# Matrix sums of a fast product moved to GpSimd, and six more chunks done as seven products

## The chip, the cores and the metric

One core of one Trainium2 chip runs the whole program. The metric is the device time of one execution in microseconds. The kernel before was timed in three runs.

## What is computed

A float32 network of three layers on 256 tokens of width 1024. The first block is feed-forward, hybrid mixer (neighbourhood attention and pooling, gated), feed-forward and a gated per-layer embedding; the second block has two layers, each with feed-forward, a mixer and feed-forward again. The first mixer of the second block is gated linear attention, the second is retention. Six feed-forward layers in all (f1, f2, s0 to s3), with hidden width 2816:

```
def swiglu(x, w_gate, w_up, w_down):
    return (jax.nn.silu(x @ w_gate) * (x @ w_up)) @ w_down

def gla_mixer(x, w_in, w_gate, b_gate, norm_g, w_out):
    q, k, v, r, g_low = split_cols(x @ w_in, GLA_SPLITS)
    log_a = log_sigmoid(g_low @ w_gate + b_gate) / GLA_TAU
    o = rms_norm_2(gla_chunked(q, k, v, log_a), norm_g)
    return (o.reshape(bsz, l, GLA_VAL) * silu(r)) @ w_out
```

Every layer ends in a residual with a normalisation, so it has to be complete before the next one begins.

## The kernel before

The 256 tokens are two tiles of 128. Activations are kept transposed (128x512 is four blocks of 128 input features for one tile) and are the stationary operand; weights stream. To get float32 accuracy, each operand is split into a high half in the fast float32 format and the rest: for weights, ScalarE casts `whi` from `raw` (L174, L196) and VectorE subtracts `wlo = raw - whi` (L177, L197). Each product is three matmuls (hi hi, hi lo, lo hi; L217 to L219), all 128x128 by 128x512.

The weights come in **units** of 128x2048 (1 MB), loaded on SP's queue, in the order of a plan that is written down once (`all_units`). A unit of a projection has four blocks of 128 rows and 512 columns. `fetch` loads and splits one; `unit` hands it to the code that uses it, and sees that the units behind it are fetched ahead (four ahead near a group of seven products). There are five buffers each for `raw`, `whi` and `wlo`, used in turn. A unit used plainly costs TensorE 2 tiles x 4 blocks x 3 = 24 matmuls.

The feed-forward layer (`ffn`) goes through its hidden columns in chunks of 512: chunks 0 to 4 with two gate units and two up units each, a chunk 5 of 256 columns, and then the down projection of 11 units (`lagged`). Some chunks are done as **seven products** (`seven`, Winograd's form of Strassen's scheme): the four weight units of a chunk are a 2x2 matrix of blocks a, b, c, d, the two tiles and the two halves of the input features the other, and seven products of 12 matmuls stand in for eight. Before, these are chunks 2 and 4 of layers f2 and s0 to s3 (`SEVEN`), the mixer's gate columns (two groups) and two pairs of retention's columns. Each product needs its own matrix: some are units, some sums of units. `fetch_sum` makes the sums in place in the `raw` buffers, one VectorE operation at L194 each, and splits the result. The seven results are added up on VectorE (L392 to L402); in the feed-forward layer the sums then give the gate, through ScalarE's Silu, and the hidden product `pr` (L476). `sums_in` makes the four differences of the inputs (`xr`, L307) and their splits.

The seven products and the plain ones are made in the same five PSUM buffers (`mm`), in turn: a product starts when the fifth product before it has been read. Work that comes later (transposes of the hidden product, for one) is put off by a count of matmul steps (`defer`, `tick`). The order on each engine is set when the program is built, and each engine then goes through its own list.

GpSimd does small things: the normalisations' powers (L247, L262, L341), the scaling of the residual (L354), the gate product of the linear attention (L799) and retention's rotation (L944, L945).

Of the kernel before, what the change touches and what calls it, by code (L numbers as in the profile page):

```python
# [35 lines left out]
SUMS = (("a", None), ("a", "b"), ("b", "c"), ("a", "c"), ("c", None), ("d", None), ("a", "d"))  # L36
# [36 lines left out]
SEVEN = (2, 4)  # L73
MIX_ORDER = [1, 0, 2, 3, (4, 5), (6, 7)]
GLA_ORDER = [1, 0, 2, 4, 3, 5]
# [16 lines left out]
class Build:  # L92
# [89 lines left out]
    def fetch_sum(self, four, j):  # L182


        nc = self.nc
        if j == 0:
            self.sums = {}
        r = self.sums
        for key, at in {0: (("a", 0), ("b", 2)), 2: (("c", 3),), 5: (("d", 1),)}.get(j, ()):
            r[key] = self.T("raw", [P, UNIT], F32)  # L190
            nc.sync.dma_start(out=r[key], in_=self.ins[four[at][0]][four[at][1]])
        key, other = SUMS[j]
        if other:
            nc.vector.tensor_tensor(out=r[key], in0=r[key], in1=r[other], op=ALU.add)  # L194
        hi, lo = self.T("whi", [P, UNIT], F32R), self.T("wlo", [P, UNIT], F32R)
        nc.scalar.copy(hi, r[key])  # L196
        nc.vector.tensor_tensor(out=lo, in0=r[key], in1=hi.bitcast(F32), op=ALU.subtract)  # L197
        return Split(hi, lo)
# [103 lines left out]
    def sums_in(self, raws, tag):  # L302

        a11, a12, a21, a22 = (raws.pop((t, n)) for t in range(NT) for n in range(2))
        y = {}
        for i, o, a, b in ((1, a22, a21, a22), (3, a21, a11, a21), (2, a11, a11, a22), (4, a12, a12, a11)):
            self.nc.vector.tensor_tensor(out=o, in0=a, in1=b, op=ALU.subtract)  # L307
# [8 lines left out]
        return y  # L316
# [52 lines left out]
    def seven(self, x, y, four, done):  # L369
# [15 lines left out]
        p1, u2, u4, c22 = t("u", "p1"), t("u", "u2"), t("y", "u4"), t("y", "c22")  # L385
        nc.scalar.copy(p1, times("P1", x[0][0], 0))
# [62 lines left out]
    def ffn(self, xT, r, wg, wu, wd, after, first=False, raws=None):  # L449
# [19 lines left out]
        def finish7(c):  # L469
            prs = []  # L470

            def done(t, a, b):
                sg = self.T("sg", [P, CW], F32)
                pr = self.T("sg", [P, CW], F32, name="pr")
                nc.scalar.activation(sg, a, AF.Silu)
                nc.vector.tensor_tensor(out=pr, in0=b, in1=sg, op=ALU.mult)  # L476
                prs.append(pr)
                if t:
                    self.defer(4, lambda: turn(c, CW, *prs))

            return done
# [35 lines left out]
        for c in range(1, 6):  # L517
            if raws is not None and c == 1:
                self.defer(4, lambda: y.update(self.sums_in(raws, "ld")))
            if raws is not None and c in SEVEN:  # L520
                self.settle(lambda: y)
# [17 lines left out]
    class Chunks:  # L539
# [10 lines left out]
        def sums(self):  # L550
            self.y.update(self.b.sums_in(self.raws, "S"))

        def pair(self, c):

            if c not in self.groups:
                self.b.settle(lambda: self.y)

                def done(t, *outs):
                    for i in range(2):
                        self.done(c[i], t, outs[i])  # L560
                        self.over.add((c[i], t))
# [210 lines left out]
    def gla(self, xT, raws, after):  # L772
# [140 lines left out]
        whole(1), ch.go(2), glow(1), ch.go(2), logits(1)  # L913
        for work in ((decay1,), (decay2,), (decay3, 0), (decay3, 1), (k_decay, 0), (k_decay, 1), (q_decay, 0), (q_decay, 1),
                     (inner, 0), (inner, 1), (far,), (read, 0, 0), (carry, 0), (read, 0, 1, read, 1, 0, carry, 1), (), (read, 1, 1)):
# [305 lines left out]
```

## Time and profile before

| | us |
|---|---|
| median of 3 runs | 1611.38 (1611.19 to 1611.48) |
| profiled execution, its own time | 1611.8 |
| its span, first to last instruction | 1610.0 |
| TensorE busy | 1589.4 |
| VectorE busy | 1233.6 |
| ScalarE busy | 836.7 |
| GpSimd busy | 107.3 |

The span is the profiled execution without what lies around it. Busy times are sums over the instructions of an engine; matmuls overlap, and so do operations that follow one another on VectorE by a little, so that a row's duration is not always the distance to the next start. In the rows below, a line is `start, duration, engine, source line, operation, output<-inputs, shapes`; a bracket at the end gives the idle time before it and what ended that.

### The profile page before, as it was taken

The numbers are of one execution on the slowest core, as the hardware profiler recorded it, in microseconds if no ns is written. First come the engines' busy times: TensorE is split into PE (matmuls) and PEld (weight loads), VectorE is DVE, ScalarE is ACT, GpSimd is POOL, SyncE is SP. The second block draws the span as 40 slices with busy tenths as digits, with TensorE's granted clock in tenths as the row PEclk, the third lists the DMA queues.
The fourth block names the chain that finished last, engine by engine and source line by source line (L and its number), as shares of the span: only waits on it lengthen the run. The fifth ranks groups of instructions, "written<-read, shape, count | busy, mean of one in ns | idle before, by whom it ended". The sixth has DMA issues, their size and how long they took to land. (4 is left out here: it accounts for less than half of the span.)

```text
span 1610.0 us, 18253 instructions
## 1 busy us (share of the span) xinstructions
PE 1589.4 (99%) x7353; PEld 1307.2 (81%) x7353; DVE 1233.6 (77%) x1086; ACT 836.7 (52%) x831; POOL 107.3 (7%) x102
## 2 busy tenths in 40 slices
PE   9999999999999999999999999999999999999997
PEld 6888877788888888888888888888887888788886
DVE  6654688978993789947648996699938899799954
ACT  7443555755663665634645563456634464456531
POOL 0000000000000100001022000100003401010000
PEclk9999999999999999999999999999999999999999
DMA  9764533654574455556534556544754543655550
GB/s 346 289 212 155 209 121 128 235 184 155 191 273 166 175 211 209 208 205 221 181 123 155 185 182 233 193 176 183 279 185 160 190 183 115 246 200 189 184 191 27
DMA packets 49797, 308.11 MB, mean 191 GB/s; under 512 B 6048, under 2 KB 7328, under 8 KB 15024
## 3 DMA queue, kind: packets, MB, share of 16 engines
q1 hardware_dynamic: 49568, 306.93, 52.6%
q8 instruction: 58, 0.95, 0.2%
q14 instruction: 27, 0.22, 0.0%
q10 hardware_dynamic: 144, 0.00, 0.0%
HBM read 305.86 MB, written 1.05 MB: 191 GB/s over the span
## 5 line engine op out<-in xcount | busy, mean ns | idle before, releaser
L177 DVE TENSOR_TENSOR wlo<-raw,whi 128x2048 fp32r<-128x2048 f32 (+1 forms) x231 | 503.1, 2185 | 247.1 <-ACT whi L174 247.0
L174 ACT CAST whi<-raw 128x2048 fp32r<-128x2048 f32 (+1 forms) x230 | 417.5, 1824 | 332.0 <-PE acc L219 190.5
L217 PE MATMUL mm<-whi,xTh 128*128 128x512 f32 x848 | 337.5, 398 | 0.2 <-ACT xTh L234 0.2
L219 PE MATMUL mm<-whi,xTl 128*128 128x512 f32 x848 | 331.4, 391 | 0.4 <-DVE xTl L235 0.4
L218 PE MATMUL mm<-wlo,xTh 128*128 128x512 f32 x848 | 331.3, 391 | 0.0
L196 ACT CAST whi<-raw 128x2048 fp32r<-128x2048 f32 x98 | 186.9, 1910 | 119.1 <-DVE raw L194 78.0
L197 DVE TENSOR_TENSOR wlo<-raw,whi 128x2048 fp32r<-128x2048 f32 x98 | 222.6, 2286 | 8.6 <-ACT whi L196 8.6
L217 PE MATMUL acc<-whi,hTh 128*128 128x512 f32 x528 | 207.0, 392 | 0.0
L219 PE MATMUL acc<-whi,hTl 128*128 128x512 f32 x528 | 205.6, 389 | 0.0
L218 PE MATMUL acc<-wlo,hTh 128*128 128x512 f32 x528 | 205.5, 389 | 0.0
L219 PEld LDWEIGHTS mm<-whi,xTl 128*128 128x128 f32 x848 | 159.2, 188 | 35.8 <-DVE xTl L235 1.8
L217 PEld LDWEIGHTS mm<-whi,xTh 128*128 128x128 f32 x848 | 159.3, 188 | 32.6 <-issue 0.8
L218 PEld LDWEIGHTS mm<-wlo,xTh 128*128 128x128 f32 x848 | 159.5, 188 | 31.1
L194 DVE TENSOR_TENSOR raw<-raw 128x2048 f32<-128x2048 f32 x56 | 128.3, 2291 | 0.1
L219 PEld LDWEIGHTS acc<-whi,hTl 128*128 128x128 f32 x528 | 99.1, 188 | 20.9
L218 PEld LDWEIGHTS acc<-wlo,hTh 128*128 128x128 f32 x528 | 99.2, 188 | 20.1
L217 PEld LDWEIGHTS acc<-whi,hTh 128*128 128x128 f32 x528 | 99.1, 188 | 20.1
L217 PE MATMUL mm<-whi,xh 128*128 128x512 f32 x176 | 69.0, 394 | 2.2 <-ACT whi L174 1.7
L218 PE MATMUL mm<-wlo,xh 128*128 128x512 f32 x176 | 68.8, 391 | 0.0
L219 PE MATMUL mm<-whi,xl 128*128 128x512 f32 x176 | 68.6, 390 | 0.0
L234 ACT CAST hTh<-hT 128x512 fp32r<-128x512 f32 (+1 forms) x72 | 38.6, 546 | 56.0 <-PE hT L226 55.8
L217 PE MATMUL P<-whi,xTh 128*128 128x512 f32 x168 | 66.3, 395 | 0.0
(261 smaller groups left out, 2105.5 us busy)
## 6 DMA issues: line engine op xcount, KB each, us to landing
raw<-in_rin SPq DMA_DIRECT2D x24, 1024.0 KB, 4.8
raw<-in_bin SPq DMA_DIRECT2D x16, 1024.0 KB, 4.8
raw<-in_f2g SPq DMA_DIRECT2D x12, 1024.0 KB, 4.8
raw<-in_s0g SPq DMA_DIRECT2D x12, 1024.0 KB, 4.8
raw<-in_gin SPq DMA_DIRECT2D x12, 1024.0 KB, 4.8
raw<-in_s1g SPq DMA_DIRECT2D x12, 1024.0 KB, 4.8
raw<-in_s2g SPq DMA_DIRECT2D x12, 1024.0 KB, 4.8
raw<-in_s3g SPq DMA_DIRECT2D x12, 1024.0 KB, 5.1
```

The source lines that it names most:

```text
L174: nc.scalar.copy(hi[:, s], raw[:, s])
L177: nc.vector.tensor_tensor(out=lo[:, s], in0=raw[:, s], in1=hi[:, s].bitcast(F32), op=ALU.subtract)
L194: nc.vector.tensor_tensor(out=r[key], in0=r[key], in1=r[other], op=ALU.add)
L196: nc.scalar.copy(hi, r[key])
L197: nc.vector.tensor_tensor(out=lo, in0=r[key], in1=hi.bitcast(F32), op=ALU.subtract)
L217: mm(ps, x.hi, w.hi, start=start, stop=False)
L218: mm(ps, x.hi, w.lo, start=False, stop=False)
L219: mm(ps, x.lo, w.hi, start=False, stop=stop)
L234: self.nc.scalar.copy(hi, v)
```

## The change

1. **Sums on GpSimd.** `fetch_sum` splits first and then adds on GpSimd (`nc.gpsimd.tensor_tensor`, new line L196), in place in the `raw` buffers. The products change their order: P1, P2, P5, P3, P7, P6, P4 with the matrices a, d, a+b, c, b+c, a+b+c, a+b+c+d. All four units of a group are now loaded with its first two products.
2. **Order of the results.** `seven` adds up in the new order (L389 to L407) and hands over each of the four results as it is complete.
3. **Input differences on GpSimd** (L316), with their splits put off by two to five steps.
4. **A third chunk:** `SEVEN` is now (2, 3, 4), so chunks 2, 3 and 4 of five feed-forward layers follow one another as groups.
5. **Linear attention:** the gate columns 4 and 5 become one group, ahead of the second half of the values (3), and the last work items are spread over the products differently.

```
-SUMS = (("a", None), ("a", "b"), ("b", "c"), ("a", "c"), ("c", None), ("d", None), ("a", "d"))
-SEVEN = (2, 4)
+SEVEN = (2, 3, 4)
-GLA_ORDER = [1, 0, 2, 4, 3, 5]
+GLA_ORDER = [1, 0, 2, (4, 5), 3]
...
-        for key, at in {0: (("a", 0), ("b", 2)), 2: (("c", 3),), 5: (("d", 1),)}.get(j, ()):
+        for key, at in {0: (("a", 0), ("b", 2)), 1: (("d", 1), ("c", 3))}.get(j, ()):
             r[key] = self.T("raw", [P, UNIT], F32)
             nc.sync.dma_start(out=r[key], in_=self.ins[four[at][0]][four[at][1]])
-        key, other = SUMS[j]
-        if other:
-            nc.vector.tensor_tensor(out=r[key], in0=r[key], in1=r[other], op=ALU.add)
+        src = r["adacbad"[j]]
         hi, lo = self.T("whi", [P, UNIT], F32R), self.T("wlo", [P, UNIT], F32R)
-        nc.scalar.copy(hi, r[key])
-        nc.vector.tensor_tensor(out=lo, in0=r[key], in1=hi.bitcast(F32), op=ALU.subtract)
+        nc.scalar.copy(hi, src)
+        nc.vector.tensor_tensor(out=lo, in0=src, in1=hi.bitcast(F32), op=ALU.subtract)
+        for o, i in {0: ("ab",), 1: ("bc",), 2: ("ac", "da")}.get(j, ()):
+            nc.gpsimd.tensor_tensor(out=r[o], in0=r[o], in1=r[i], op=ALU.add)
...
-        for i, o, a, b in ((1, a22, a21, a22), (3, a21, a11, a21), (2, a11, a11, a22), (4, a12, a12, a11)):
-            self.nc.vector.tensor_tensor(out=o, in0=a, in1=b, op=ALU.subtract)
...
+        for n, (i, o, a, b) in enumerate(((1, a22, a21, a22), (3, a21, a11, a21), (2, a11, a11, a22), (4, a12, a12, a11))):
+            self.nc.gpsimd.tensor_tensor(out=o, in0=a, in1=b, op=ALU.subtract)
+            self.defer(2 + n, lambda i=i, o=o: split(i, o))
...
+        u2, c11, c12, c22 = t("u", "u2"), t("u", "c11"), t("y", "c12"), t("y", "c22")
+        nc.scalar.copy(u2, times("P1", x[0][0], 0))
         yield
-        p5 = times("P5", y[1], 1)
+        TT(out=c11, in0=times("P2", x[0][1], 1), in1=u2, op=ALU.add)
+        done(0, 0, c11)
         yield
-        p7 = times("P7", y[3], 2)
+        self.settle(lambda: len(y) == 4)
+        p5 = times("P5", y[1], 2)
         yield
-        TT(out=u2, in0=times("P6", y[2], 3), in1=p1, op=ALU.subtract)
-        TT(out=u4, in0=p5, in1=u2, op=ALU.add)
-        TT(out=c22, in0=u4, in1=p7, op=ALU.subtract)
+        p3 = times("P3", y[4], 3)
+        yield
+        p7 = times("P7", y[3], 4)
+        yield
+        TT(out=u2, in0=times("P6", y[2], 5), in1=u2, op=ALU.subtract)
+        TT(out=c12, in0=p5, in1=u2, op=ALU.add)
+        TT(out=c22, in0=c12, in1=p7, op=ALU.subtract)
         TT(out=u2, in0=u2, in1=p7, op=ALU.subtract)
-        yield
-        TT(out=u4, in0=times("P3", y[4], 4), in1=u4, op=ALU.add)
-        yield
-        TT(out=p1, in0=times("P2", x[0][1], 5), in1=p1, op=ALU.add)
-        done(0, p1, u4)
+        TT(out=c12, in0=p3, in1=c12, op=ALU.add)
+        done(0, 1, c12)
+        done(1, 1, c22)
         yield
         TT(out=u2, in0=times("P4", x[1][1], 6), in1=u2, op=ALU.subtract)
-        done(1, u2, c22)
+        done(1, 0, u2)
...
-        whole(1), ch.go(2), glow(1), ch.go(2), logits(1)
+        whole(1), ch.go(2), glow(1), ch.go(1), self.defer(4, ch.sums), ch.go(1), logits(1)
```

**VectorE, between two groups of layer s1.** Before, from the last splits of chunk 2's group into plain chunk 3 (`L197` splits a matrix of a group, `L177` a plain unit; P_6900 is P6, P_6845 P5, P_6882 P7, P_6923 P3, P_6943 P2):

```order
L197 TENSOR_TENSOR wlo<-raw,whi 128x2048 x3
L235 TENSOR_TENSOR hTl<-hT,hTh 128x512
L177 TENSOR_TENSOR wlo<-raw,whi 128x2048
L235 TENSOR_TENSOR hTl<-hT,hTh 128x512
L392 TENSOR_TENSOR u_6824<-P_6900,p_6823 128x512
L177 TENSOR_TENSOR wlo<-raw,whi 128x2048
L393 TENSOR_TENSOR u_6825<-P_6845,u_6824 128x512
L177 TENSOR_TENSOR wlo<-raw,whi 128x2048
L394 TENSOR_TENSOR c_6826<-u_6825,P_6882 128x512
L395 TENSOR_TENSOR u_6824<-u_6824,P_6882 128x512
L397 TENSOR_TENSOR u_6825<-P_6923,u_6825 128x512
```

And now, from chunk 2's group into chunk 3's (`L194` is now the split of a group's matrix; P_7022 is P6, P_6961 P5, P_7000 P7, P_6978 P3, P_7048 P4; the row of three is the last split of chunk 2 and the first two of chunk 3):

```order
L194 TENSOR_TENSOR wlo<-raw,whi 128x2048 x3
L399 TENSOR_TENSOR u_6901<-P_7022,u_6901 128x512
L194 TENSOR_TENSOR wlo<-raw,whi 128x2048
L400 TENSOR_TENSOR c_6903<-P_6961,u_6901 128x512
L194 TENSOR_TENSOR wlo<-raw,whi 128x2048
L401 TENSOR_TENSOR c_6904<-c_6903,P_7000 128x512
L402 TENSOR_TENSOR u_6901<-u_6901,P_7000 128x512
L403 TENSOR_TENSOR c_6903<-P_6978,c_6903 128x512
L407 TENSOR_TENSOR u_6901<-P_7048,u_6901 128x512
L484 TENSOR_TENSOR pr<-c_6903,sg 128x512
```

The operations that read P5 (L400) and P3 (L403) stand behind the splits of the third and the fourth matrix of the next group, which before were splits of plain units. The third matrix is a sum.

**GpSimd, around one feed-forward layer of the second block (s1 and s2 look alike).** Before, GpSimd had only the normalisations there (two `rl` and four scalings for each layer's end):

```order
L341 TENSOR_TENSOR rl<-mv,mhalf 128x1
L354 TENSOR_SCALAR h_86<-y 128x512 x2
L341 TENSOR_TENSOR rl<-mv,mhalf 128x1
L354 TENSOR_SCALAR h_87<-y 128x512 x2
L341 TENSOR_TENSOR rl<-mv,mhalf 128x1
```

And now, behind the same operations of one layer's end and ahead of those of the next:

```order
L355 TENSOR_SCALAR h_87<-y 128x512 x2
L316 TENSOR_TENSOR xr<-xr 128x512 x4
L196 TENSOR_TENSOR raw<-raw 128x2048 x12
L342 TENSOR_TENSOR rl<-mv,mhalf 128x1
L355 TENSOR_SCALAR h_86<-y 128x512 x2
```

Each feed-forward layer has four input differences and then twelve sums there, four for each group, each waiting for the split that reads the buffer before it is overwritten. Over the program there are 80 sums at L196 where there were 56 at L194, 331 splits of 128x2048 where there were 313, and 6396 matmuls of split operands where there were 6468.

## Rows read from the trace of the kernel before

**Rows 1.** The page, busy us, share of the span and instructions of three engines.
```profile
PE 1589.4 (99%) x7353; PEld 1307.2 (81%) x7353; DVE 1233.6 (77%) x1086; ACT 836.7 (52%) x831; POOL 107.3 (7%) x102
```

**Rows 2.** Busy time by engine in stretches: mixer, linear attention, third feed-forward layer, parts, retention.
```profile
core 0: us, PE busy (x) PEld busy (x) DVE busy (x) ACT busy (x) POOL busy (x), PEclk, DMA share, GB/s
205.00:350.00 145.00, 140.90 (x690) 113.97 (x690) 124.30 (x123) 81.80 (x106) 0.55 (x1) 0.99 0.46 170
765.00:855.00 90.00, 90.00 (x446) 74.19 (x445) 52.12 (x54) 49.48 (x67) 11.89 (x16) 1.00 0.42 146
872.00:1036.00 164.00, 164.00 (x748) 135.83 (x748) 127.32 (x98) 85.19 (x69) 0.27 (x2) 1.00 0.53 192
885.00:965.00 80.00, 80.00 (x369) 66.36 (x368) 75.46 (x51) 46.50 (x37) 0.00 (x0) 1.00 0.50 183
965.00:1036.00 71.00, 71.00 (x321) 58.74 (x320) 40.69 (x36) 28.00 (x21) 0.15 (x1) 1.00 0.61 220
1310.00:1413.00 103.00, 101.86 (x459) 82.98 (x458) 89.95 (x83) 51.44 (x44) 9.82 (x12) 1.00 0.57 208
```

**Rows 3.** Timeline of TensorE in a plain chunk: start us, duration us.
```profile
899.82 0.39 PE L217 MATMUL mm<-whi,xTh 128*128 128x512 f32 x1
900.05 0.39 PE L218 MATMUL mm<-wlo,xTh 128*128 128x512 f32 x1
...
901.64 0.39 PE L219 MATMUL mm<-whi,xTl 128*128 128x512 f32 x1
```

**Rows 4.** Groups of instructions by shape: busy us, mean ns | idle before, releasers.
```profile
L177 DVE TENSOR_TENSOR wlo<-raw,whi 128x2048 fp32r<-128x2048 f32 x215 | 493.0, 2297 | 245.5 <-ACT whi L174 245.5
L174 ACT CAST whi<-raw 128x2048 fp32r<-128x2048 f32 x215 | 408.7, 1908 | 330.5 <-PE acc L219 190.5 <-PE mm L219 62.2 <-issue 33.2
L194 DVE TENSOR_TENSOR raw<-raw 128x2048 f32<-128x2048 f32 x56 | 128.3, 2291 | 0.1
L458 DVE TENSOR_TENSOR pr<-mm,sg 128x512 f32<-128x512 f32 x30 | 20.6, 687 | 13.6 <-PE mm L219 13.4
```

**Rows 5.** Timeline of GpSimd: undisturbed two-input operations of three sizes.
```profile
805.37 1.29 POOL L799 TENSOR_TENSOR gate<-gate,gnorm 128x512 f32<-128x512 f32 x1 [0.77 <-ACT gate L798]
...
1233.53 0.72 POOL L945 TENSOR_TENSOR rot<-rb,ra 128x256 f32<-128x256 f32 x1
...
1294.28 0.56 POOL L247 TENSOR_TENSOR rr<-err,mhalf 128x1 f32<-128x1 f32 x1
```

**Rows 6.** Groups of GpSimd: all four gate products together.
```profile
L799 POOL TENSOR_TENSOR gate<-gate,gnorm 128x512 f32<-128x512 f32 x4 | 6.1, 1516 | 47.1 <-ACT gate L798 47.1
```

**Rows 7.** Timeline of VectorE and GpSimd side by side, at two places.
```profile
1037.84 3.84 POOL L354 TENSOR_SCALAR h<-y 128x512 f32<-128x512 f32 x2 [1.01 <-DVE y L349]
1038.33 2.29 DVE L177 TENSOR_TENSOR wlo<-raw,whi 128x2048 fp32r<-128x2048 f32 x1
1040.53 0.69 DVE L235 TENSOR_TENSOR xTl<-xT,xTh 128x512 fp32r<-128x512 f32 x1
...
1243.39 2.83 DVE L177 TENSOR_TENSOR wlo<-raw,whi 128x2048 fp32r<-128x2048 f32 x1
...
1247.34 5.02 DVE L177 TENSOR_TENSOR wlo<-raw,whi 128x2048 fp32r<-128x2048 f32 x2
1247.56 2.65 POOL L944 TENSOR_TENSOR rot<-ra,rb 128x256 f32<-128x256 f32 x1 [3.49 <-DVE rb L941]
1250.17 2.78 POOL L945 TENSOR_TENSOR rot<-rb,ra 128x256 f32<-128x256 f32 x1
```

**Rows 8.** Timeline of TensorE behind its longest wait.
```profile
283.94 1.98 PE L696 MATMUL py<-pl,pool_w 128*128 128x256 f32 x4 [3.54 <-ACT pl L592]
...
286.14 0.63 PE L218 MATMUL P<-wlo,xTh 128*128 128x512 f32 x1
286.56 0.63 PE L219 MATMUL P<-whi,xTl 128*128 128x512 f32 x1
```

**Rows 9.** Busy time in the 2 us behind that wait, columns as in rows 2.
```profile
284.00:286.00 2.00, 2.00 (x5) 1.64 (x6) 2.00 (x5) 0.41 (x2) 0.00 (x0) 0.52 0.00 0
```

**Rows 10.** DMA issues of the page: KB each, median us to landing.
```profile
raw<-in_s1g SPq DMA_DIRECT2D x12, 1024.0 KB, 4.8
```

More of the change, by code (lines that the diff above doesn't have):

```diff
@@ L300, in turn_in, with sums_in, split @@
         self.defer(TURN[t] + n + (more if raws is not None else 0), turn)
-    def sums_in(self, raws, tag):
+    def sums_in(self, raws, tag, y):
         a11, a12, a21, a22 = (raws.pop((t, n)) for t in range(NT) for n in range(2))
-        y = {}
-        for i, o, a, b in ((1, a22, a21, a22), (3, a21, a11, a21), (2, a11, a11, a22), (4, a12, a12, a11)):
-            self.nc.vector.tensor_tensor(out=o, in0=a, in1=b, op=ALU.subtract)
+        def split(i, o):
             if i < 3:
@@ L315, in sums_in @@
             y[i] = Split(hi, lo)
-        return y
+        for n, (i, o, a, b) in enumerate(((1, a22, a21, a22), (3, a21, a11, a21), (2, a11, a11, a22), (4, a12, a12, a11))):
+            self.nc.gpsimd.tensor_tensor(out=o, in0=a, in1=b, op=ALU.subtract)
+            self.defer(2 + n, lambda i=i, o=o: split(i, o))
     def rms_post(self, t, acc, gpost, half):
@@ L469, in finish7, with done @@
         def finish7(c):
[L470 to L479, printed above, removed]
+            got, prs = {}, {}
+            def done(t, i, ps):
+                got[t, i] = ps
+                if i == 0:
+                    sg = got[t, 0] = self.T("sg", [P, CW], F32)
+                    nc.scalar.activation(sg, ps, AF.Silu)
+                if (t, 1 - i) in got:
+                    prs[t] = pr = self.T("sg", [P, CW], F32, name="pr")
+                    nc.vector.tensor_tensor(out=pr, in0=got[t, 1], in1=got[t, 0], op=ALU.mult)
+                if t and i == 0:
+                    self.defer(4, lambda: turn(c, CW, prs[0], prs[1]))
             return done
@@ L518, in ffn @@
             if raws is not None and c == 1:
-                self.defer(4, lambda: y.update(self.sums_in(raws, "ld")))
+                self.defer(4, lambda: self.sums_in(raws, "ld", y))
             if raws is not None and c in SEVEN:
-                self.settle(lambda: y)
                 for _ in self.seven(xT, y, [(wg, 2 * c), (wg, 2 * c + 1), (wu, 2 * c), (wu, 2 * c + 1)], finish7(c)):
@@ L550, in sums, with done @@
         def sums(self):
-            self.y.update(self.b.sums_in(self.raws, "S"))
+            self.b.sums_in(self.raws, "S", self.y)
         def pair(self, c):
             if c not in self.groups:
[L556 to L561, printed above, removed]
+                def done(t, i, ps):
+                    self.done(c[i], t, ps)
+                    self.over.add((c[i], t))
                 self.groups[c] = self.b.seven(self.xT, self.y, [(self.name, 2 * i + j) for i in c for j in range(2)], done)
@@ L912, in gla @@
         whole(0), ch.go(3), glow(0), ch.go(1), logits(0)
-        whole(1), ch.go(2), glow(1), ch.go(2), logits(1)
+        whole(1), ch.go(2), glow(1), ch.go(1), self.defer(4, ch.sums), ch.go(1), logits(1)
         for work in ((decay1,), (decay2,), (decay3, 0), (decay3, 1), (k_decay, 0), (k_decay, 1), (q_decay, 0), (q_decay, 1),
-                     (inner, 0), (inner, 1), (far,), (read, 0, 0), (carry, 0), (read, 0, 1, read, 1, 0, carry, 1), (), (read, 1, 1)):
+                     (inner, 0), (inner, 1), (far,), (read, 0, 0), (carry, 0), (read, 0, 1), (read, 1, 0, carry, 1), (read, 1, 1)):
             i = 0
```

2 lines of the change are left out of this document (removed).

## Prediction

> **What bounds the kernel now.** I read the page's busy times first. TensorE is busy 1589.4 of 1610.0 us, VectorE 1233.6, GpSimd 107.3 [rows 1]. Next come the stages. In the third feed-forward layer, 872 to 1036 us, TensorE has no gap at all; but in its chunks 1 to 4, 885 to 965 us, VectorE is busy 75.46 of 80.00 us, in the 71 us of down projection behind them 40.69 [rows 2]. So TensorE sets the time, and VectorE follows so closely in just the stretch that the change rewrites. Last, a matmul's listed duration is no price: matmuls overlap, and the starts of neighbours lie 0.228 us apart (899.82 to 901.64, eight matmuls later) [rows 3]. I count that for each.
>
> **Products.** A plain chunk of four weight units costs 4 x 24 = 96 matmuls; as seven products it costs 7 x 12 = 84. Six chunks more are done so (chunk 3 in five layers, the gates once): 72 matmuls x 0.228 = **16.4 us off TensorE**, all on the path.
>
> **Splits.** Each new group splits seven matrices where four were split: 18 casts x 1.91 us on ScalarE and 18 subtractions on VectorE [rows 4]. ScalarE is busy 46.50 of 80.00 us in the stretch [rows 2], which hides its share: nothing. If that cover were gone it would be 34 us. The subtractions are in the account below.
>
> **Sums.** The 56 in-place sums at L194, 2.29 us each [rows 4], leave VectorE, and 80 appear on GpSimd (20 groups x 4). The trace has no GpSimd operation of 128x2048. An undisturbed two-input one takes 0.72 us at 128x256 and 1.29 at 128x512 [rows 5], 0.57 more for 256 columns; six more such lots give **4.7**, which I take as the nearest. Bounds: counting from the 128x1 operation at 0.56 [rows 5], 1.29 + 3 x 0.73 = 3.5; four times the mean of all four gate products (1.52) [rows 6], some of which were disturbed, 6.1. Taken alone, 4 x 4.7 = 18.8 us in a group of seven products (7 x 12 x 0.228 = 19.2 us) would just fit.
>
> **They don't run alone.** At 1247.34 two subtractions (whi from raw, both inputs in SBUF) stand on VectorE, and two rotation products on GpSimd arrive among them. The first needs 2.65 us instead of about 0.72: it waits for the running subtraction. It then runs, and the pair of subtractions takes 5.02 instead of 2 x 2.29, 0.45 more: the second one stood still until GpSimd was through; the second rotation again takes 2.78 [rows 7]. At 1037.84 a GpSimd scaling sits out the whole subtraction behind it, 3.84 us for two of them, while the subtraction takes its plain 2.29 and the xTl operation behind it, which has an input in PSUM, its plain 0.69 [rows 7]. So GpSimd and VectorE exclude each other wherever VectorE reads two operands from SBUF; with one in PSUM it doesn't. What the rows don't show is a long GpSimd operation with a subtraction arriving early in it. The longest such wait is 0.54 us (2.83 against 2.29 at 1243.39) [rows 7]. Bounds for what a sum of 4.7 us does to a waiting subtraction: 0.54 us, or all 4.7. I take all of it, because in each row VectorE stood until the GpSimd operation ended.
> The Trainium skill, page SBUF — State Buffer, section Who interferes with whom, speaks against the change in the same way: a VectorE instruction with two SBUF inputs and a GpSimd one that reads SBUF take a shared port pair in turn, and the later one blocks for the whole instruction. By that rule the sum is the one below; by waits of 0.54 us it would be that of the first rival.
>
> **Feed-forward layers.** Sums and subtractions then use one resource in turn. Per group: 7 subtractions x 2.2 (their starts back to back, 1038.33 to 1040.53 [rows 7]) + 4 sums x 4.7 + 2 operations on the hidden product, both inputs in SBUF, x 0.69 [rows 4] = 15.4 + 18.8 + 1.4 = **35.6 us, against 19.2 us of TensorE**. Before, a plain chunk (4 x 24 x 0.228 = 21.9 us of TensorE) stood between two groups and let VectorE catch up; now chunks 2, 3 and 4 follow each other. The first group can be prepared during chunk 1: five buffers of each split half allow splitting from 21.9 us before its first product, and its four sums and seven subtractions (34.2 us) end about when they are needed. The second and third can't: 2 x (35.6 - 19.2) = **33 us** of waiting.
> Walking the new order of the queues through adds to it. On VectorE the subtraction of the second group's third matrix stands ahead of the operation that frees P5's PSUM buffer, in which the next group's P1 is to be made, and one more ahead of that which frees P3's, for P2. Both subtractions wait for a sum, so TensorE first waits some 12 us at the second group's P1 and 5 at its P2, later 4 to 5 us at each of P1, P2 and the transposes of the third. Behind the third group, the raw buffer of its first matrix is held until the sixth split, so the next unit's load (4.8 us to land [rows 10]) starts late, and VectorE's queue puts three subtractions ahead of the freeing operation: up to 9 more, 42 in all. I take **36 us per layer, 180 for five**. With 3.5 us per sum the rate gives 23 (115); with 6.1, 44 (220).
>
> **Mixer and retention.** Their four groups exist already; 16 sums go from 2.29 to 4.7 us of the shared resource, 39 us. VectorE's idle time there is 145.00 - 124.30 = 20.7 us and 103.00 - 89.95 = 13.1 us [rows 2]. I take 12, bounds 0 and 39. The linear attention has room (52.12 of 90.00 us busy [rows 2]) for 3 subtractions and 4 sums, 25 us; its decay chain may wait behind a sum, and the last values are read right after they are made: 3, bounds 0 and 10.
>
> **At nothing:** the operand differences (28 of L307 on VectorE, now 32 on GpSimd at 1.29 us): they run during chunk 1, ahead of the group's sums; without that cover, 4 x 1.29 = 5.2 us a call. Also the clock: after TensorE waited 3.54 us at 283.94, the grant was 0.52 of full speed in the 2 us behind, and starts lay 0.42 apart instead of 0.228 [rows 8, 9]: 1.2 GHz for about 2 us, some 1 us lost. Where TensorE waits for sums anyway that loss is hidden; uncovered, some four such waits in five layers are 20.
>
> **Sum.** Against the profiled execution's 1611.8: - 16.4 + 180 + 12 + 3 = 1790.4; the median of the runs is 0.4 lower, so I say **1790 us**. Low ends: 1611.4 - 16.4 + 115 = 1710. High ends: 1611.4 - 16.4 + 220 + 39 + 10 + 20 = 1884.
>
> **Rivals.**
> *Faster: the exclusion costs little.* If a waiting subtraction gets in between parts of a long GpSimd operation, a sum costs VectorE at most 0.54 us. Then three groups need 21 x 2.2 of subtractions, 21 operations on products and 12 others at 0.69 (hidden products and their splits) and 12 x 0.54: 46.2 + 22.8 + 6.5 = 75.5 us, against 57.5 us of products plus some 14 us in stock (five units x 2.7): 4 us late per layer at worst, most likely 1. 1611.4 - 16.4 + 3 = **1598**. For it: four sums fit in 19.2 us; VectorE loses 56 x 2.29 = 128 us. Against: no row shows VectorE getting in. It decides between waits of under about 1 us and the whole operation. Chance 0.16. With 4 us late in each layer and little else it ends at 1611 to 1615, no change: 0.03.
> *Half.* The exclusion holds but more is prepared ahead than I count, or a sum is nearer 3 us: 10 to 20 us a layer, 1611.4 - 16.4 + 75 = **1670**. Against: buffers for five units only. Chance 0.07.
> *Worse.* The waits feed each other also in the mixers, each late PSUM buffer delaying splits by their buffers: 44 a layer and the high ends of the others, **1884** and more. Against: in the mixers, attention work on TensorE lies between. Chance 0.04.
> *The change doesn't do what it says:* the order shows 80 sums on GpSimd, none on VectorE, 72 matmuls fewer; no chance left.
>
> **How the numbers follow.** The forecast has 0.70. Over 0.2% (3.2 us, about what a measurement can tell) slower: 0.70 + 0.07 + 0.04 = 0.81; within: 0.03; faster: 0.16. The range leaves out the faster and unchanged cases (0.19) and reaches over the others: from 1640, the foot of the half case, to the high ends, 1880. The forecast's own range is 1710 to 1880.
>
> **What would show it.** In the changed profile: sums on GpSimd near 4.7 us undisturbed and near 6.9 with a subtraction ahead; subtractions up to 4.7 us longer than 2.29, alternating with sums; TensorE gaps of several us, at the second and third group of every feed-forward layer, put down to VectorE's product operations or subtractions; the layer's stretch 30 us longer, the down projection unchanged; matmuls 72 fewer at the same pitch. Wrong, if subtractions beside sums keep 2.29 to 2.9 us: then the first rival. If the sums take 4.7 but TensorE's gaps lie elsewhere, the walk is wrong and the rate right.

## The result and the profile after

The changed kernel takes **1864.43 us** (median of 4 runs, 1863.01 to 1864.99), the one before 1611.29 (1611.17 to 1611.48) beside it: a ratio of **1.157 [1.155, 1.159]**, 253 us more. The forecast was 1790, its range 1640 to 1880. Of the spans of the two profiled executions the difference is 251.2.

The page of the profile after, busy us by engine (before: [rows 1]):

```profile
PE 1650.0 (89%) x7281; PEld 1337.7 (72%) x7281; DVE 1391.0 (75%) x1066; ACT 870.7 (47%) x859; POOL 604.2 (32%) x214
```

The 72 matmuls are gone, and TensorE is still busy 61 us longer; the other 190 us of the longer span are gaps. Where the time went is read by stage, from the second layer norm's small GpSimd operation at the end of one layer to the first at the end of the next (in the first block, between the like operations of its own normalisation). Layer s1 is the third of the five feed-forward layers that the change touches (f2, s0 to s3), and is called the third one here. These two rows of GpSimd's timeline bound it, 208.53 us apart; before they stood 167.35 apart.

```profile
975.08 0.99 POOL L342 TENSOR_TENSOR rl<-mv,mhalf 128x1 f32<-128x1 f32 x1 [7.97 <-DVE mv L341]
...
1183.61 0.99 POOL L342 TENSOR_TENSOR rl<-mv,mhalf 128x1 f32<-128x1 f32 x1 [87.79 <-DVE mv L341]
```

All stages so: the five feed-forward layers are 42.3, 39.9, 41.2, 42.0 and 42.2 us longer, together **207.6**; the mixer 7.4, the linear attention 17.2, the retention 20.4, together **45.0**. The rest didn't move.

Within that layer, the whole, the stretch with the three groups and the down projection (columns as in [rows 2]):

```profile
979.00:1184.00 205.00, 173.16 (x736) 140.32 (x735) 153.99 (x96) 90.14 (x73) 76.64 (x17) 0.92 0.42 153
1006.00:1125.00 119.00, 87.19 (x348) 69.44 (x347) 103.80 (x59) 52.75 (x40) 61.49 (x11) 0.86 0.42 157
1125.00:1184.00 59.00, 58.97 (x265) 48.55 (x264) 27.26 (x23) 20.11 (x17) 0.39 (x1) 1.00 0.46 159
```

The down projection has no gap. In the 119 us ahead of it TensorE stands still for 31.8, and its granted clock has a mean of 0.86 where it was 1.00: 348 matmuls take 87.19 us, 0.251 each, against 80.00 / 369 = 0.217 in [rows 2], both stretches with 28 short transposes among them. (1.00 is 2.4 GHz; the mean lies between that and the lower level, 1.2.) The clock isn't low throughout. These two pieces, columns as above, lie behind a gap of 2.29 us and behind one of 8.22:

```profile
1036.00:1040.00 4.00, 2.97 (x12) 2.18 (x12) 0.80 (x2) 0.00 (x0) 4.00 (x1) 1.00 0.00 0
1048.00:1053.00 5.00, 4.86 (x13) 3.89 (x14) 5.00 (x1) 0.95 (x1) 4.92 (x2) 0.57 0.00 0
```

TensorE's longest groups of waits (us in total, times, longest):

```profile
PE hT L225 <- DVE pr L484: 54.3, 10, 6.4
PE P L216 <- DVE c L400: 36.2, 5, 8.2
PE P L216 <- DVE u L402: 26.7, 5, 5.6
PE mm L216 <- DVE u L399: 20.6, 5, 4.1
PE tp L225 <- DVE kend L855: 14.7, 1, 14.7
```

The first four occur once or twice in each of the five layers and all wait for VectorE. Now the two groups of instructions that share the resource (busy us, mean ns):

```profile
L196 POOL TENSOR_TENSOR raw<-raw 128x2048 f32<-128x2048 f32 x80 | 440.8, 5509 | 275.3 <-DVE wlo L194 272.2
L194 DVE TENSOR_TENSOR wlo<-raw,whi 128x2048 fp32r<-128x2048 f32 x140 | 466.9, 3352 | 67.3 <-ACT whi L193 66.9
```

A subtraction took 2.297 us before [rows 4]; these 140 take 3.35. And the passage from the first of the three groups into the second, in the timeline (start, duration; VectorE, GpSimd, ScalarE, and TensorE's waits; a row with x2 is two operations on end):

```profile
1034.08 11.15 POOL L196 TENSOR_TENSOR raw<-raw 128x2048 f32<-128x2048 f32 x2 [8.43 <-DVE wlo L194]
1036.12 0.68 DVE L399 TENSOR_TENSOR u<-P,u 128x512 f32<-128x512 f32 x1
1036.95 0.47 PE L216 MATMUL P<-whi,xTh 128*128 128x512 f32 x1 [2.29 <-DVE u L399]
...
1040.67 3.70 ACT L193 CAST whi<-raw 128x2048 fp32r<-128x2048 f32 x2 [7.94 <-POOL raw L196]
1042.60 4.79 DVE L194 TENSOR_TENSOR wlo<-raw,whi 128x2048 fp32r<-128x2048 f32 x1 [5.80 <-ACT whi L193]
...
1047.31 0.68 DVE L400 TENSOR_TENSOR c<-P,u 128x512 f32<-128x512 f32 x1
1047.47 4.54 POOL L196 TENSOR_TENSOR raw<-raw 128x2048 f32<-128x2048 f32 x1 [2.24 <-DVE wlo L194]
1047.91 6.25 DVE L194 TENSOR_TENSOR wlo<-raw,whi 128x2048 fp32r<-128x2048 f32 x1
1048.14 0.77 PE L216 MATMUL P<-whi,xTh 128*128 128x512 f32 x1 [8.22 <-DVE c L400]
...
1052.05 1.91 ACT L193 CAST whi<-raw 128x2048 fp32r<-128x2048 f32 x1 [4.40 <-POOL raw L196]
1052.09 6.44 POOL L196 TENSOR_TENSOR raw<-raw 128x2048 f32<-128x2048 f32 x1
1054.09 0.68 DVE L401 TENSOR_TENSOR c<-c,P 128x512 f32<-128x512 f32 x1
...
1056.48 2.61 DVE L484 TENSOR_TENSOR pr<-c,sg 128x512 f32<-128x512 f32 x1
...
1071.34 11.19 POOL L196 TENSOR_TENSOR raw<-raw 128x2048 f32<-128x2048 f32 x2 [12.81 <-DVE wlo L194]
```

The two sums from 1047.47 on read like this. The first takes 4.54 and ends at 1052.01. The subtraction that arrives at 1047.91 stands until then and runs 2.15: it ends at 1054.16, 6.25 us after its start. The second sum waits for that end and runs 4.4, to 1058.53. The hidden product at 1056.48, both operands in SBUF, waits for 1058.53 in turn and takes 2.61 instead of 0.69. Each waits for the whole of the other. Meanwhile the operations with one operand in PSUM (L401 and three more, between 1054.09 and 1056.56) take their plain 0.68. TensorE's 8.22 us at the second group's P2 are the chain sum, cast, subtraction (4.79, half of it blocked), and only then L400, which frees its PSUM buffer. The next group's sums start 1071.34 - 1034.08 = **37.3 us** later, in which four sums, seven subtractions and two hidden products make some 34.6 us of work (4 x 4.5 + 7 x 2.2 + 2 x 0.6); TensorE needs 19.2.

The buffers do not come in turn, as the part on the kernel before has it. The second group's P1 starts at 1036.95, 0.15 us behind L399, which reads P6, and 10.4 us before L400 reads P5, the fifth product before it. It is P2 that waits for L400.

### The profile page after: what moved, and what is told of

It reads as the page before. It is cut to its first block, busy times and chain, and to the rows that moved or that the text cites. A ratio compares the mean times of both kernels' runs of the same rounds, so it can differ in the third digit from the quotient of the medians.

```text
span 1861.2 us, 18435 instructions
## 1 busy us (share of the span) xinstructions
PE 1650.0 (89%) x7281; PEld 1337.7 (72%) x7281; DVE 1391.0 (75%) x1066; ACT 870.7 (47%) x859; POOL 604.2 (32%) x214
## 5 line engine op out<-in xcount | busy, mean ns | idle before, releaser
L176 DVE TENSOR_TENSOR wlo<-raw,whi 128x2048 fp32r<-128x2048 f32 (+1 forms) x207 | 449.4, 2184 | 276.4 <-ACT whi L173 276.3
L173 ACT CAST whi<-raw 128x2048 fp32r<-128x2048 f32 (+1 forms) x206 | 371.8, 1813 | 373.9 <-PE acc L218 199.8
L196 POOL TENSOR_TENSOR raw<-raw 128x2048 f32<-128x2048 f32 x80 | 440.8, 5509 | 275.3 <-DVE wlo L194 272.2
L194 DVE TENSOR_TENSOR wlo<-raw,whi 128x2048 fp32r<-128x2048 f32 x140 | 466.9, 3352 | 67.3 <-ACT whi L193 66.9
L193 ACT CAST whi<-raw 128x2048 fp32r<-128x2048 f32 x140 | 264.9, 1903 | 324.2 <-POOL raw L196 234.7
L216 PE MATMUL mm<-whi,xTh 128*128 128x512 f32 x656 | 267.5, 408 | 20.8 <-DVE u L399 20.6
L218 PE MATMUL mm<-whi,xTl 128*128 128x512 f32 x656 | 262.8, 401 | 0.4 <-DVE xTl L234 0.4
L217 PE MATMUL mm<-wlo,xTh 128*128 128x512 f32 x656 | 261.4, 399 | 0.0
L217 PE MATMUL P<-wlo,xTh 128*128 128x512 f32 x240 | 100.4, 418 | 3.6 <-DVE wlo L194 3.6
L218 PE MATMUL P<-whi,xTl 128*128 128x512 f32 x240 | 99.2, 413 | 0.0
```

The source lines that it names most:

```text
L173: nc.scalar.copy(hi[:, s], raw[:, s])
L176: nc.vector.tensor_tensor(out=lo[:, s], in0=raw[:, s], in1=hi[:, s].bitcast(F32), op=ALU.subtract)
L193: nc.scalar.copy(hi, src)
L194: nc.vector.tensor_tensor(out=lo, in0=src, in1=hi.bitcast(F32), op=ALU.subtract)
L196: nc.gpsimd.tensor_tensor(out=r[o], in0=r[o], in1=r[i], op=ALU.add)
L216: mm(ps, x.hi, w.hi, start=start, stop=False)
```

## The experiments

The theory was that GpSimd's sums and VectorE's operations with two SBUF operands exclude each other, so that a group takes 37 us where TensorE needs 19.2. Rival A: the sum is merely long, and the cast behind it waits. Rival B: three groups in a row are too much, whoever makes the sums. Results first; differences from the kernel before in us, by stage from each profile. e3, e4, e5 and e9 leave the true sums out of the products and e12 the true lower halves of the weights; they stand for their times alone.

| run | median us | ratio to before | five feed-forward layers | mixer | linear attention | retention |
|---|---|---|---|---|---|---|
| the change | 1864.43 | 1.157 [1.155, 1.159] | +207.6 | +7.4 | +17.2 | +20.4 |
| e3 sums as traffic only | 1872.32 | 1.162 [1.160, 1.164] | +201.6 | +12.9 | +7.4 | +32.8 |
| e8 sums in quarters | 1898.13 | 1.177 [1.175, 1.179] | +244.5 | +2.2 | +17.5 | +21.1 |
| e1 sums on VectorE | 1740.61 | 1.080 [1.078, 1.081] | +107.6 | +3.3 | +10.2 | +8.5 |
| e2 two chunks | 1728.86 | 1.072 [1.070, 1.074] | +73.0 | +9.3 | +17.2 | +19.8 |
| e9 three fills for a sum | 1687.21 | 1.047 [1.045, 1.048] | +63.4 | -3.4 | +4.2 | +13.1 |
| e12 one operand | 1676.29 | 1.040 [1.038, 1.042] | +41.5 | +0.8 | +12.3 | +10.5 |
| e4 two fills for a sum | 1657.35 | 1.028 [1.027, 1.030] | +27.3 | +3.3 | +5.6 | +9.4 |
| e5 no sums | 1635.19 | 1.014 [1.011, 1.017] | +13.1 | +2.6 | +5.3 | +5.3 |
| e7 two chunks, sums on VectorE | 1632.67 | 1.013 [1.011, 1.014] | 0.0 | +3.1 | +9.0 | +9.7 |
| e10 also differences on VectorE | 1630.32 | 1.011 [1.010, 1.013] | +0.1 | +2.7 | +7.9 | +8.8 |
| e11 e7 with plain gates | 1623.74 | 1.007 [1.006, 1.009] | 0.0 | +3.1 | +0.1 | +10.6 |
| e6 before, with the gates' group | 1616.23 | 1.003 [1.002, 1.004] | +0.1 | 0.0 | +8.3 | -0.7 |

**e1: the sums on VectorE.**

```
-            nc.gpsimd.tensor_tensor(out=r[o], in0=r[o], in1=r[i], op=ALU.add)
+            nc.vector.tensor_tensor(out=r[o], in0=r[o], in1=r[i], op=ALU.add)
```

> The changed kernel with its 80 sums on VectorE instead of GpSimd; order, third chunk and gates stay. Theory (GpSimd's sums and VectorE's two-SBUF-operand instructions take turns on one resource): the sums then cost 2.29 us each instead of 4.5 to 6.6, and nothing stands still, but VectorE gets 17.8 us more work per feed-forward layer (3 subtractions x 2.2, 4 sums x 2.29, 3 products' operations x 0.69) in a stretch of 77 us where it was busy 75: 13 to 16 us of waits per layer, no loss in the mixer, the retention and the linear attention. About 1670 us (1640 to 1690). Rival A (only the length of a GpSimd sum, for which the cast behind it waits, is the cause): 1595 to 1605. Rival B (the third group of seven without a plain chunk between is the cause, whoever makes the sums): feed-forward layers stay 40 us longer than before, 1800 or more.

1740.6, 50 above the expected range and 60 below rival B's: half of the feed-forward loss went with the engine alone, and the other stages lost 22.0 instead of 45.0. Rival A is out, and rival B holds for the other half: the third chunk cost 21.5 us per layer, more than expected. This row of chunks 1 to 4 of the third layer says why:

```profile
942.00:1042.00 100.00, 89.00 (x379) 71.11 (x378) 98.38 (x68) 57.61 (x45) 0.51 (x1) 0.95 0.44 157
```

VectorE is busy 98.38 of 100.00 us (before, 75.46 of 80 [rows 2]): it is the bound, with no GpSimd in it.

**e3: the sums as traffic only.**

```
-            nc.gpsimd.tensor_tensor(out=r[o], in0=r[o], in1=r[i], op=ALU.add)
+            nc.gpsimd.tensor_tensor(out=self.spare, in0=r[o], in1=r[i], op=ALU.add)
```

> The changed kernel with the GpSimd sums kept as traffic only: each reads the same two raw units but writes a spare bf16 tile, and nobody waits for it; the products are made of unsummed units (two buffers of the small SBUF pool make room for the spare tile). The casts no longer wait for a sum. Theory (exclusion): each sum still blocks VectorE's subtractions for its 4.5 us, 35 us of the shared resource per group against 19.2 of TensorE, so most of the loss stays: 1770 to 1860 us, subtractions up to 6.7 us long, TensorE's waits at the second and third group. Rival A (the wait of the cast for the sum is the cause): the loss is gone, 1595 to 1610, although subtractions may read longer. Rival B (the third group itself): unchanged, about 1860, but with subtractions near 2.29.

As slow as the change and 12 us above the theory's upper end, although no cast waits for a sum. GpSimd's and VectorE's groups of e3, and the stretch with the three groups of the third layer (columns as in [rows 2]):

```profile
L196 POOL TENSOR_TENSOR spare<-raw 128x2048 bf16<-128x2048 f32 x80 | 444.0, 5550 | 277.8 <-DMA raw<-in_f2u 39.5 <-DMA raw<-in_s2u 36.1 <-DMA raw<-in_rin 36.0
```

```profile
L194 DVE TENSOR_TENSOR wlo<-raw,whi 128x2048 fp32r<-128x2048 f32 x140 | 517.7, 3718 | 9.2 <-ACT whi L193 9.0
```

```profile
1000.00:1120.00 120.00, 85.45 (x364) 68.55 (x364) 119.66 (x58) 53.88 (x40) 63.90 (x11) 0.89 0.39 142
```

The subtractions hardly wait for a cast any more (9.0 us instead of 66.9) and take 3.72 us instead of 2.30, and VectorE, its blocked time counted, is busy 119.66 of 120.00 us. Exclusion alone is enough for the loss in the feed-forward layers: e5 below, with neither sums nor traffic, loses 13.1 there. (A sum still holds the raw units that it reads, so loads can wait for it; the fills of e9, below, hold their target units too and cost far less. The two buffers given up for the spare tile may be what the mixer and the retention lose here beyond the change; that was not tried.)

**e4 and e9: GpSimd writes and doesn't read.**

```
-            nc.gpsimd.tensor_tensor(out=r[o], in0=r[o], in1=r[i], op=ALU.add)
+            for _ in range(2):
+                nc.gpsimd.memset(r[o], 0.01)
```

> The changed kernel with each GpSimd sum replaced by two fills of the whole target unit with a constant, on GpSimd: the casts still wait for GpSimd, but it reads nothing from SBUF; the products are made of constants where sums stood. The length of a fill isn't known here; two were taken so as to keep GpSimd's latency near a sum's. Theory (exclusion by operands read): subtractions keep 2.29 us, a group costs VectorE 15.4 + 6 us, and the loss is gone but for a few us: 1595 to 1620. Rival A (latency of GpSimd in the chain): with pairs of fills at 4 to 5 us, 1800 to 1860 as before. If fills also block subtractions (then they read up to 6 us long), the run says only that writing takes the resource too.

1657 us, 37 above what the theory expected at most, and far from rival A's 1800. A fill takes 1.81 us, so two were shorter than a sum; e9 repeats it with three.

> The changed kernel with three fills in the place of each sum (two of them took 3.6 us, less than a sum; three take 5.44, about the 5.5 us that a sum takes in the changed kernel); the products are made of constants where sums stood. The casts wait for GpSimd as long as in the changed kernel, but GpSimd reads nothing and subtractions stay undisturbed. Theory (exclusion): some us per layer more than with two fills, 1665 to 1700. Rival A (latency of GpSimd in the chain of sum, cast and subtraction): 1800 to 1870.

```profile
L197 POOL MEMSET raw<- 128x2048 f32 x240 | 432.4, 1813 | 193.1 <-DVE wlo L194 108.4 <-DMA raw<-in_rin 22.6 <-DMA raw<-in_bin 12.5
```

```profile
L194 DVE TENSOR_TENSOR wlo<-raw,whi 128x2048 fp32r<-128x2048 f32 x140 | 318.5, 2295 | 77.6 <-ACT whi L193 76.8
```

GpSimd is as busy as with sums (432.4 against 440.8 us), the casts still wait for it (78.9 us in all, against 234.7 in the changed kernel, whose sums also wait for subtractions), and a subtraction takes its plain 2.295 us. 91 of the 140 run while a fill does, and these take 2.273 to 2.295: both engines write 128x2048 side by side, and it costs the subtraction nothing. The loss in the feed-forward layers falls from 207.6 to 63.4: without exclusion rival A's latency is worth 63.4 - 13.1 (e5) = 50.

**e5: no sums at all.**

```
-            nc.gpsimd.tensor_tensor(out=r[o], in0=r[o], in1=r[i], op=ALU.add)
+            pass
```

> The changed kernel without the sums: the products are made of unsummed units, everything else stays (21 subtractions and casts for three groups, the third chunk, the differences on GpSimd, the gates as seven products). Theory and rival A: the whole loss lies in the sums, -16.4 us of products remain: 1595 to 1605. Rival B (the third group of seven and its subtractions): feed-forward layers still over 10 us longer than before each, 1650 or more.

A miss by 30 us. Even with the sums gone each feed-forward layer is 2.6 us longer than before instead of 2.7 shorter. In the third layer TensorE waits 2.1 us for a cast and 1.6 for L399. (e5's four runs spread over 10 us; even the fastest, 1630.35, is above the expected range.) So with 21 subtractions close together the third chunk wouldn't have paid even if the sums were free.

**e8: the sums in quarters.**

```
+            for p in range(0, UNIT, CW):
+                nc.gpsimd.tensor_tensor(out=r[o][:, p:p + CW], in0=r[o][:, p:p + CW], in1=r[i][:, p:p + CW], op=ALU.add)
```

> The changed kernel with each GpSimd sum written as four of 128x512: the same work, but VectorE can get in between pieces. Theory (the amount of work on the shared resource decides): four pieces take 4 x 1.29 = 5.2 us instead of 4.5, a group 15.4 + 20.7 + 1.4 = 37.5 us: 1850 to 1890, subtractions no more than about 1.3 to 3 us longer than 2.29. Rival (granularity: subtractions stuck behind a whole sum of 4.5 us, and the queue behind them, are what hurts): with waits of at most 1.3 us two thirds of the loss go, 1680 to 1750.

```profile
L197 POOL TENSOR_TENSOR raw<-raw 128x512 f32<-128x512 f32 x320 | 569.5, 1816 | 202.2 <-DVE wlo L194 202.2
```

```profile
L194 DVE TENSOR_TENSOR wlo<-raw,whi 128x2048 fp32r<-128x2048 f32 x140 | 363.5, 2611 | 129.2 <-ACT whi L193 128.4
```

VectorE does get in between the pieces: a subtraction takes 2.61 us in the mean and never over 3.5. But now the sum waits at each piece (4 x 1.816 = 7.3 us for a sum), and the kernel is slower than the change, 8 us above the expected range, in which a piece was reckoned at 1.29. Letting VectorE in between doesn't make the work of the two less, and doesn't help.

**e12: one operand on VectorE.** The sums stay on GpSimd; the 140 subtractions become reductions that read 128x2048 elements of one tensor instead of two; they write 128x512.

```
-        nc.vector.tensor_tensor(out=lo, in0=src, in1=hi.bitcast(F32), op=ALU.subtract)
+            nc.vector.tensor_reduce(out=lo[:, :CW], in_=hi.bitcast(F32).rearrange("p (n k) -> p n k", k=4), axis=AX.X, op=ALU.add)
```

> The changed kernel, GpSimd sums and all, but the 140 subtractions of the seven-product groups are reductions on VectorE that read the same 128x2048 elements as one operand (the cast half alone) and write 128x512; the lower halves of the products' weights are thus other numbers. The casts still wait for the sums, the products for VectorE. What such a reduction takes alone isn't known here; near 2.2 us makes the run comparable. Theory (VectorE and GpSimd exclude each other only where VectorE reads two operands from SBUF): sums near 4.5 us and reductions undisturbed by each other; what is left is the sums' latency, between the runs with fills of 3.6 and 5.4 us: 1640 to 1700. Rival (any reading of SBUF by VectorE excludes GpSimd): 1780 to 1870, reductions up to 6.7 us long.

```profile
L195 DVE TENSOR_REDUCE wlo<-whi 128x512 fp32r<-128x2048 f32 x140 | 317.2, 2276 | 46.3 <-ACT whi L193 45.7
```

```profile
L198 POOL TENSOR_TENSOR raw<-raw 128x2048 f32<-128x2048 f32 x80 | 381.5, 4775 | 166.7 <-ACT whi L193 163.7
```

All 140 take between 2.261 and 2.290 us beside 80 real sums, 53 of them wholly within one, and the feed-forward loss is 41.5. With the same sums on GpSimd and VectorE's operation as long, one operand fewer takes away four fifths of the loss. (A sum no longer waits for a subtraction to have read its target; that shortens the chain somewhat, so not all of it need be the exclusion. That the reduction also writes a quarter as much isn't parted from it here; e9 shows that writing alone doesn't block.)

**e2 and e7: two chunks**, the sums on GpSimd (e2) and on VectorE (e7, with e1's edit too).

```
-SEVEN = (2, 3, 4)
+SEVEN = (2, 4)
```

> The changed kernel without its third chunk: chunks 2 and 4 as seven products, chunk 3 plain between them; the sums stay on GpSimd. Theory (sums and subtractions in turn on one resource, 37 us per group where TensorE needs 19.2, and three groups in a row leave no time to catch up): a plain chunk adds 21.9 us of TensorE and some 10 of the resource, so 81 us of demand stand against some 79 us to the last subtraction: 2 to 10 us lost per feed-forward layer instead of 41; the mixer, the linear attention and the retention keep their +45. About 1685 us (1665 to 1710). Rival (each group with GpSimd sums costs by itself, a third of the layer's 41 us, wherever it stands): 1611 + 45 + 5 x 27 = about 1790.

> The changed kernel with two chunks of seven products and with its sums on VectorE: what is left of the change is the new order of the products, the differences on GpSimd and the gates as seven products. Theory (sums on GpSimd and the third chunk are the whole loss in the feed-forward layers; the rest has a price of its own, since with the sums left out the mixer, linear attention and retention were still 13 us longer, with the sums on VectorE 22): feed-forward layers within 3 us of before, mixer, linear attention and retention +15 to +22: 1625 to 1635. Rival (those stages lost time only through the sums, and the order is free): 1605 to 1612.

e2 lost 14.6 us per layer, not 2 to 10, and lies 19 above its range: a plain chunk between two groups doesn't make up for 37 us. TensorE's waits in e2 lie behind the groups, where the operations that free its buffers stand behind late subtractions:

```profile
PE hT L225 <- DVE pr L484: 22.6, 9, 4.0
PE mm L216 <- DVE u L399: 22.6, 5, 4.5
```

e7 came out as expected: the feed-forward layers are at 0.0, and 21.7 us are left elsewhere. Four runs tell the two halves of the change apart in the feed-forward layers. With neither the sums on GpSimd nor the third chunk the loss is 0.0 (e7), with the sums alone 73.0 (e2), with the third chunk alone 107.6 (e1), with both 207.6, which is 27 more than the two losses added.

**e10, e11 and e6: what is left.** e10 is e7 with the differences back on VectorE, e11 is e7 with plain gates and the old work list, and e6 is the kernel before with only the gates' group and its work list.

```
-            self.nc.gpsimd.tensor_tensor(out=o, in0=a, in1=b, op=ALU.subtract)
+            self.nc.vector.tensor_tensor(out=o, in0=a, in1=b, op=ALU.subtract)
```

> The changed kernel with two chunks, sums on VectorE and also the differences of the input on VectorE: of the change the order of the products and the gates remain. Without this last edit it took 1632.7 us, 21.8 of them in the mixer, the linear attention and the retention. Theory (the differences on GpSimd, at 1.3 to 1.9 us each and behind other work in its queue, come late for the products and hold up GpSimd's rotations): 10 to 15 us come back, 1618 to 1623. Rival (order of the products and gates cause it): 1630 to 1634.

```
-GLA_ORDER = [1, 0, 2, (4, 5), 3]
+GLA_ORDER = [1, 0, 2, 4, 3, 5]
```

> The changed kernel with two chunks, sums on VectorE and plain gates (also the order of the linear attention's steps as before): the differences on GpSimd and the order of the products remain. Theory (the gates' group costs the linear attention some 9 us, a stage that had no wait before): 1632.7 - 9 = 1622 to 1625, linear attention at 93 us again, mixer and retention still 3 and 10 longer. Rival (gates as seven products are worth their 2.7 us, and the stage lost through what comes before): 1632 to 1636.

```
-GLA_ORDER = [1, 0, 2, 4, 3, 5]
+GLA_ORDER = [1, 0, 2, (4, 5), 3]
```

> The kernel before with the gates of the linear attention as seven products and nothing else of the change: sums and differences on VectorE, old order of the products, two chunks in the feed-forward layers. It could beat both kernels. 12 matmuls fewer give -2.7 us if VectorE's 3 subtractions, 4 sums and 4 differences (some 18 us) find room in the linear attention, where VectorE was busy 53 of 93 us: 1608 to 1610. Rival (the group's late operands and VectorE's queue delay the decay chain behind it, as in the run with two chunks and sums on VectorE, where that stage was 9 us longer): 1613 to 1621.

e10: a miss, and its rival came out. The differences on GpSimd cost 2.4 us by the medians, and the two intervals overlap; the retention stays 8.8 us longer and the mixer 2.7. e11 came out as expected: the linear attention is back at +0.1. e6: its rival came out; the gates' group alone makes that stage 8.3 us longer. So the gates are not worth their 2.7 us in either kernel, and none of the versions tried beats the one before. The stage before, and in e6 (columns as in [rows 2]):

```profile
759.20:852.60 93.40, 93.40 (x471) 76.64 (x470) 53.42 (x59) 48.23 (x67) 13.10 (x17) 1.00 0.47 163
759.20:860.60 101.40, 95.92 (x457) 77.10 (x457) 75.88 (x79) 55.95 (x75) 15.26 (x17) 0.95 0.42 149
```

Before it had no gap there; now 5.5 us are gaps, and fewer matmuls take 2.5 us more at a mean clock of 0.95. Its longest wait there is 2.4 us, for an operation of the decay chain.

By elimination, the retention's 8.8 us and the mixer's 2.7 in e10 belong to the new order of the products and results with what came with it: splits put off, sums made behind the splits, units loaded earlier. Nothing else of the change is left there. Which piece of it was not tried apart.

## Why the prediction was right, and where it was too small

**Right: the direction and its cause.** The step on which all hung, that a waiting subtraction stands for the *whole* GpSimd operation and not for the longest wait that the rows showed (0.54 us), is what the timeline after shows (6.25 = 4.10 of waiting + 2.15). Subtractions reach 6.70 us, sums 6.60 (7.0 and 6.9 foretold). And e3, e9 and e12 show from three sides that it makes the loss: traffic without a wait keeps it, a wait without reading loses most of it, one operand fewer on VectorE too. The first rival fell with it.

**Right: the price of a sum.** 4.7 us were estimated from two smaller sizes; the shortest are 4.514, the median with waits is 4.99.

**The group's period**: 35.6 us predicted, 37.3 between the first sums of the second group and of the third.

**Where the gaps lie: the sum near, the places only in part.** The walk gave P1 of the second group the buffer of P5 and P2 that of P3, by the rule of five buffers in turn; the trace has P1 behind P6 and P2 behind P5. So P1 waits only 2.29, behind the subtractions of the first two matrices; the wait for the third one's, 12 us at P1 in the walk, is the 8.22 at P2; and the fourth one's, 5 us at P2 in the walk, holds up no product, but the hidden product behind it, for which the transposes in the second group wait 5.00, a place that was not named. In the third group the walk put 4 to 5 at each of P1, P2 and the transposes; P1 and P2 don't wait, P5 waits 5.56, the transposes 6.26. Behind it 4.13 were measured, 9 at most predicted. All gaps of the stretch are 31.8, against the 33 that the rate gave and the 36 that were taken. The rate gives the number; the walk's places don't.

**Too small: the feed-forward layers**, the first term mis-sized: 36 us per layer, 180 in all, 166 with the saved products. Measured are 207.6, or 44 per layer before the saving, the upper bound of the range (220). In the third layer 31.8 of it are the waits; what came on top is the step "clock: nothing". In the stretch TensorE's 348 matmuls took 0.034 us more each, 11.7 us, at a mean granted clock of 0.86, with five gaps of 4.1 to 8.2 us among them: some 2.3 us behind each, where the prediction reckoned 1 and took it to be hidden under the waits. Gaps and slower matmuls together make the 43.5. How much would remain at full clock was not tried. And not all of it is the move to GpSimd: the third chunk has a price of its own. The first rival counted 1 us late per layer if the sums cost little, but e5, without any sums, misses the saving of 2.7 us by 5.4 per layer (2.6 longer instead of 2.7 shorter), and e1, with sums on VectorE, is 21.5 longer than before.

**Too small: the linear attention**, 3 predicted, 0.3 net of the products; 17.2 measured. "Room" was read from a busy share (52.12 of 90 us). The sums on GpSimd cost 17.2 - 9.0 (e7) = 8.2 of it; TensorE's one long wait of 14.7 us on `kend`, an operation of the decay chain, is in both kernels with GpSimd sums (the change, e2) and in neither with VectorE's (e1, e7). Operations of that chain read two operands from SBUF as well (L838, L840), and the sums block them. Their rows in the change, and below the gap one of each in e7:

```profile
884.98 5.70 DVE L838 SCALAR_TENSOR_TENSOR zb<-zb,ze 128x512 f32<-128x512 f32 x2
890.61 6.63 DVE L840 TENSOR_TENSOR_SCAN ze<-reset,zb 128x512 f32<-128x512 f32 x2
...
796.80 0.68 DVE L838 SCALAR_TENSOR_TENSOR zb<-zb,ze 128x512 f32<-128x512 f32 x1
799.61 1.21 DVE L840 TENSOR_TENSOR_SCAN ze<-reset,zb 128x512 f32<-128x512 f32 x1
```

Two of each take 12.3 us where undisturbed ones would take 3.8: 8.5 us more, about the 8.2. The gates' group alone, with its sums on VectorE, costs 8.3 (e6). That there too the place decides, because the group's operands come due right ahead of the decay chain, is argued from TensorE's waits and not tried apart.

**Too small: mixer and retention**, 12 predicted, 27.8 measured. The sums account for (7.4 - 3.1) + (20.4 - 9.7) = 15, near the 12. The other 12.8 (3.1 + 9.7 in e7) are a step that was missing: the new order of the products, with what came with it, got no price of its own there.

The three terms, 41, 17 and 16 us, make the 74 between 1790 and 1864. The measured time lies 16 us below the top of the range. That top was made of sums of 6.1 us, the high ends of the other stages and 20 us of uncovered clock loss; here the sums took about the 4.7 foretold, and the clock and the price of the new order filled the room. That the time falls within the range is in that part luck. **Casts at nothing** held in the main: ScalarE's busy time rose by the 34 us predicted, but a cast of 1.91 us stands in P2's chain above, and e5 waits 2.1 us for one. The differences at nothing held, as far as can be told (2.4 us, e10 against e7, with the sums on VectorE). The last rival, waits that feed one another into the mixers at 1884, is near in number and not the cause: the mixer lost 7.4.

## What to carry to other kernels

Add up VectorE's operations with two SBUF operands and GpSimd's operations that read SBUF as *one* queue before moving work from the one to the other: here each sum moved made that queue 2.2 us longer, and a group with 35 us of such work fed a TensorE that needed 19. VectorE, at 94% in the stretch before, couldn't take a denser version of it, whoever made the sums: without any sums the third chunk still lost. And a stage with idle time isn't a stage with room: ask whether the work comes due just ahead of a chain, and whether the chain's own operations read two operands from SBUF.

## What the runs showed of the chip

- A blocked operation stands until the other has ended and then runs for about its own time (2.28 us a subtraction, 4.51 a sum, undisturbed), in both directions. In the changed kernel 46 subtractions of 128x2048 arrived in a running sum; all ended 2.15 us behind it (2.146 to 2.159). 36 sums arrived in a running subtraction; all ended 4.35 to 4.49 us behind it. Cutting the GpSimd operation in four turned part of the waits over to GpSimd (1.82 instead of 1.29 us per piece in e8).
- GpSimd fills of 128x2048 (1.81 us each) leave a two-operand subtraction at 2.295 us, and a VectorE reduction over one operand (2.261 to 2.290 us in all 140) isn't touched by GpSimd's sums. The Trainium skill, page SBUF — State Buffer, section Who interferes with whom, says both: VectorE's second SBUF input contends with a GpSimd instruction that reads, not with one that only writes, and a VectorE instruction with one input outside its two-port modes doesn't contend. These runs agree.
- Gaps cost more than their length: 31.8 us of gaps in 119 came with a mean grant of 0.86 and 11.7 us of slower matmuls. Behind the gap of 8.22 us matmuls took 0.63 us each for a while and started 0.43 apart instead of 0.23; behind the one of 2.29 us the clock stayed at 1.00.
